# Dense projections on Trainium2: both parts of x as one operand of 512 columns, weights in 512 by 512 pieces

## The chip, the core and the metric

The kernel runs on one core of one Trainium2 chip. The time is the device time of one execution in microseconds (us); the median of several runs is compared. A core has a matrix engine (TensorE, PE in the profile, with its weight loads as PEld), a vector engine (VectorE, DVE), a scalar engine (ScalarE, ACT), GpSimd (POOL) and SyncE (SP), which issues nearly all DMAs here. Each engine works through a queue of its own in order and waits where another engine, or a DMA, has not yet delivered.

## What is computed

A trunk of two layers over x of 256 tokens by 1024 channels, float32 throughout. Each layer is a mixer and a feed-forward part, each followed by a residual and a layer norm:

```python
for l in range(DEPTH):                       # 2 layers
    h = x @ w_in[l]                          # 1024 -> 2304 columns
    q, k, v, u, xr, xg = jnp.split(h, IN_SPLITS, axis=-1)   # 512, 512, 512, 256, 256, 256
    y_attn = _diff_attention(q, k, v, lam, ...)             # 4 heads, softmax of two maps, p0 - lam * p1
    y_pool = _pool_mixer(u, pool_w[l], pool_scale[l])       # windows of 2, 4, 8 and 16
    y_lru = _rglru_mixer(xr, xg, ...)                       # convolution, gated scan, times gelu(xg)
    mix = jnp.concatenate([y_attn, y_pool, y_lru], axis=-1) @ w_out[l]
    x = _layer_norm(alpha * x + mix, ln1_g[l], ln1_b[l])
    if l % 2 == 0:
        f = _swiglu(x, ffn_w_gate, ffn_w_up, ffn_w_down)    # 1024 -> 2816 -> 1024
    else:
        f = _moe_swiglu(x, router_w, ...)                   # 8 experts of that size, 2 for each token
    x = _layer_norm(alpha * x + f, ln2_g[l], ln2_b[l])
```

## The kernel before

A float32 product is made of three products in a faster number type of the matrix engine (fp32r). Every operand is kept as two parts: `hi`, the value rounded to that type, and `lo`, what is left of it. A product is hi by hi, plus lo by hi, plus hi by lo; `mm3` issues these three matmuls. A weight tile comes by DMA as `raw`; `weight` makes `hi` with a ScalarE copy (L112) and `lo` with a VectorE subtraction (L114), for half a tile of 128x1024 at a time. x stands turned (channels on the partitions, 256 tokens along the row) in two tiles, `xh` and `xl`, made by `new_xT`.

A mixer goes in this order: values (`project_values`, which for layer 0 is `project_first_values`), then seven calls of `project` for 256 columns of `w_in` each: the recurrent channels xr, two for the queries (qT), two for the keys (kT), the gate branch xg and the pooling channels up. `project` takes two blocks c of 128 columns; for each block it goes over eight k (128 channels each) and issues `mm3` with the weights as the fixed operand and x as the moving one, 256 columns wide (L144, L145, L146). The two blocks share one PSUM bank, and one ScalarE copy of 128x512 brings the result to SBUF. Values and the first two chunks of the feed-forward part use `project_rows`: here x is the fixed operand, for 128 tokens t, and the weights move, 256 columns at a time.

Around the projections of the mixer stand the recurrent gates and the scan; the scores `sc` (L437; b is the block of 128 queries, and for b = 0 all four heads of one map fit in one bank of 128x512); the softmax (mask L451, row maximum L452, its scaling `nm` L453, exponentials on ScalarE L455, the ratio of the two maps L459 to L461, the difference `pr` L463); the turning of the probabilities (L504, copied by ScalarE as `pT`, L505) and their product with the values (L509); the gelu of xg on VectorE and ScalarE (L418 to L423); then the pooling sums and the output projection.

The feed-forward part of layer 0 (`dense_ffn`) has 11 chunks of 256 columns: two by `rows_part`, nine by `up_part`, where silu and the product of gate and up read PSUM. Layer 1 streams the weights of eight experts, 277 MB, through a ring of raw tiles, and a part of them is asked for while the mixer of layer 1 is still at work.

The order of the work is made by a scheduler when the program is built: it gives each engine its queue, from the order of the code, the data and the buffers. Pools of few buffers bound it: `mmp` has three PSUM banks for projections, `accp` four (scores and output projection), `tpp` one; the raw ring has five tiles at first, the split parts six or eight.

## Time and profile before

| | us |
|---|---|
| runs | 1109.02, 1110.88, 1113.15 |
| median | 1110.88 |
| the profiled execution, its own time | 1113.36 |
| its span, first to last instruction | 1111.6 |
| PE busy | 1067.3 (96%) |
| weight loads busy | 788.6 (71%) |
| DVE busy | 654.5 (59%) |
| ACT busy | 518.6 (47%) |
| mean granted TensorE clock | 0.977 of full |
| DMA | 346.9 MB, 312 GB/s |

The busy shares are means over stages that differ. In the order of time: from 0 to about 108 us the mixer of layer 0; to about 300 us the feed-forward part, in which PE has no gap; to about 400 us the mixer of layer 1; then the router, and from 420 us on the experts, in which the DMA engines are busy all the time. A row of a timeline is a start, a duration, the engine, the line of the program, the operation, what it writes and reads, and its form; in brackets stands the idle time ahead of it and what ended that. A matmul's duration holds its way through the array, and the next one starts earlier, so the pace of a stream of matmuls is read from starts.

### The profile page before, as it was taken

The numbers are of one execution on the slowest core, as the hardware profiler recorded it, in microseconds if no ns is written. First come the engines' busy times: TensorE is split into PE (matmuls) and PEld (weight loads), VectorE is DVE, ScalarE is ACT, GpSimd is POOL, SyncE is SP. The second block draws the span as 40 slices with busy tenths as digits, with TensorE's granted clock in tenths as the row PEclk, the third lists the DMA queues.
The fourth block names the chain that finished last, engine by engine and source line by source line (L and its number), as shares of the span: only waits on it lengthen the run. The fifth ranks groups of instructions, "written<-read, shape, count | busy, mean of one in ns | idle before, by whom it ended". The sixth has DMA issues, their size and how long they took to land. (4 is left out here: it accounts for less than half of the span.)

```text
span 1111.6 us, 15280 instructions
## 1 busy us (share of the span) xinstructions
PE 1067.3 (96%) x5866; PEld 788.6 (71%) x5867; DVE 654.5 (59%) x869; ACT 518.6 (47%) x722; POOL 24.8 (2%) x65
## 2 busy tenths in 40 slices
PE   8989999999998999999999999999999999999994
PEld 8977999999898883467873347884346884355883
DVE  6777744554777650169862049872138892137896
ACT  5865444444457330156651046761036772135773
POOL 1001000000100100000000000000000000000000
PEclk9989999999998969999999999999999999999998
DMA  9733755555473728999999999999999999999951
GB/s 311 291 112 113 265 168 181 190 184 189 127 263 141 261 117 350 414 413 413 409 419 419 414 414 412 406 419 398 386 414 411 409 420 371 374 412 412 411 208 41
DMA packets 152546, 346.91 MB, mean 312 GB/s; under 512 B 8196, under 2 KB 57488, under 8 KB 152464
## 3 DMA queue, kind: packets, MB, share of 16 engines
q1 hardware_dynamic: 152288, 345.56, 81.6%
q8 instruction: 48, 0.79, 0.3%
q14 instruction: 34, 0.28, 0.1%
q10 hardware_dynamic: 144, 0.26, 0.1%
q0 software_dynamic: 32, 0.02, 0.0%
HBM read 344.77 MB, written 1.05 MB: 311 GB/s over the span
## 5 line engine op out<-in xcount | busy, mean ns | idle before, releaser
L114 DVE TENSOR_TENSOR lo<-raw,hi 128x1024 fp32r<-128x1024 f32 x380 | 446.8, 1221 | 143.8 <-ACT hi L112 143.2
L112 ACT CAST hi<-raw 128x1024 fp32r<-128x1024 f32 x380 | 375.9, 1049 | 124.5 <-issue 54.3
L144 PE MATMUL mm<-xh,hi 128*128 128x256 f32 x512 | 147.1, 288 | 0.0
L145 PE MATMUL mm<-xh,lo 128*128 128x256 f32 x512 | 146.0, 285 | 0.0
L146 PE MATMUL mm<-xl,hi 128*128 128x256 f32 x512 | 146.0, 285 | 0.0
L1004 DVE TENSOR_TENSOR sg<-pu,sg 128x512 f32<-128x512 f32 (+2 forms) x36 | 23.3, 647 | 164.4 <-PE pu L976 137.8
L959 PE MATMUL pg<-hi,xg 128*128 128x512 f32 (+1 forms) x384 | 97.0, 378 | 4.7 <-ACT hi L112 4.7
L144 PEld LDWEIGHTS mm<-xh,hi 128*128 128x128 f32 x512 | 99.5, 195 | 0.9
L145 PEld LDWEIGHTS mm<-xh,lo 128*128 128x128 f32 x512 | 99.6, 194 | 0.4
L146 PEld LDWEIGHTS mm<-xl,hi 128*128 128x128 f32 x512 | 99.4, 194 | 0.0
L959 PE MATMUL pu<-hi,xg 128*128 128x512 f32 (+1 forms) x384 | 95.0, 373 | 0.0
L1028 PE MATMUL py<-hi,hT 128*128 128x512 f32 x344 | 92.9, 392 | 0.0
L976 PE MATMUL pg<-raw,xs 128*64 128x512 f32 (+1 forms) x384 | 86.2, 571 | 0.0
L976 PE MATMUL pu<-raw,xs 128*64 128x512 f32 (+1 forms) x384 | 84.3, 561 | 0.0
L959 PEld LDWEIGHTS pg<-hi,xg 128*128 128x128 f32 x384 | 68.4, 190 | 22.0 <-ACT hi L112 8.1
L998 PE MATMUL py<-raw,hs 128*64 128x512 f32 x352 | 79.9, 598 | 0.0
L959 PEld LDWEIGHTS pu<-hi,xg 128*128 128x128 f32 x384 | 68.3, 189 | 13.5 <-issue 0.7
L1003 ACT ACTIVATE sg<-pg 128x512 f32<-128x512 f32 (+2 forms) x36 | 20.3, 563 | 118.5 <-PE pg L976 69.6
L1028 PEld LDWEIGHTS py<-hi,hT 128*128 128x128 f32 x344 | 64.0, 188 | 13.6
L976 PEld LDWEIGHTS pg<-raw,xs 128*64 128x64 f32 x384 | 26.3, 139 | 44.8 <-issue 41.7
L976 PEld LDWEIGHTS pu<-raw,xs 128*64 128x64 f32 x384 | 26.2, 137 | 43.9 <-issue 41.6
L961 PE MATMUL pg<-lo,xg 128*128 128x512 f32 (+1 forms) x192 | 56.6, 383 | 0.6 <-DVE lo L114 0.4
(297 smaller groups left out, 1271.4 us busy)
## 6 DMA issues: line engine op xcount, KB each, us to landing
raw<-in_moe_w_down_dram SPq DMA_DIRECT2D x87, 1024.0 KB, 12.9
raw<-in_moe_w_gate_dram SPq DMA_DIRECT2D x76, 1024.0 KB, 14.2
raw<-in_moe_w_up_dram SPq DMA_DIRECT2D x76, 1024.0 KB, 13.6
raw<-in_w_in_dram SPq DMA_DIRECT2D x17, 1024.0 KB, 5.5
raw<-in_moe_w_gate_dram SPq DMA_DIRECT2D x16, 768.0 KB, 9.4
raw<-in_moe_w_up_dram SPq DMA_DIRECT2D x16, 768.0 KB, 8.3
raw<-in_ffn_w_gate_dram SPq DMA_DIRECT2D x11, 1024.0 KB, 5.1
raw<-in_ffn_w_up_dram SPq DMA_DIRECT2D x11, 1024.0 KB, 5.2
```

The lines of the kernel that those rows point to most:

```text
L112: act.copy(hi, raw[:, s, :])
L114: last_lo[:] = [vec.tensor_sub(lo, raw[:, s, :], hi.bitcast(F32))]
L144: pe.matmul(ps, lh, rh, start=first, stop=False)
L145: pe.matmul(ps, ll, rh, start=False, stop=False)
L146: return pe.matmul(ps, lh, rl, start=False, stop=last)
L959: pe.matmul(ps[:, :n], xg[i][:, k0 + k, :], w[k][0], start=(k0 + k + i == 0), stop=False)
L961: pe.matmul(ps[:, :n], xg[0][:, k0 + k, :], w[k][1], start=False, stop=(k0 + k == KD - 1))
L976: pe.matmul(ps[h * HALF:(h + 1) * HALF, :n], xs[:, k0 + k, :], raw[:, k, h * n:(h + 1) * n], start=(k0 + k == 0), stop=(k0 + k == KD - 1))
L998: pe.matmul(py[nn * HALF:(nn + 1) * HALF, :], hs[:, k % nk, k // nk, :], raw[:, k - k0, nn * 512:(nn + 1) * 512], start=(f + k == 0), stop ...
L1003: act.activation(sg[:, :n], pg[:, :n], AF.Silu)
L1004: vec.tensor_mul(sg[:, :n], pu[:, :n], sg[:, :n])
L1028: pe.matmul(ps, hT[i][:, k0 + k, :], w[k][0][:, s], start=(first and i == 0), stop=False)
```

## The change

`new_xT` makes one tile `x2`, with hi and lo of x beside each other for each k. `project` now issues two matmuls where it had three: the weight's hi part against the 512 columns [hi | lo] of x, and the weight's lo part against the 256 columns of x's hi. Both land in one bank of 128x512 for each block c: the left half takes hi by hi and lo by hi, the right half takes hi by lo. The two halves have to be added: a ScalarE copy of the right half (128x256) to the destination, then a VectorE addition of the left half to it. So a call of `project` takes two banks in turn instead of one, and ends with two copies and two additions instead of one copy. In `up_part` silu and the product with the up half now read SBUF, and a tile `su` is added.

`project_rows` takes weights 512 columns wide and half of the channels (`k0`) at a call. The weight pieces for values and for the first chunks are 512 rows by 512 columns instead of 1024 by 256, so a DMA row is 2 KB instead of 1 KB, at the same bytes for a piece. Counted over the program: 32 calls of `project` had 1536 matmuls of 256 columns, and have 512 of 512 columns and 512 of 256; `project_rows` had 384 of 256 columns and has 192 of 512. The 64 blocks have 64 copies and 64 additions. The layer norm's factors `g_b` of layer 1 take a tile of the raw ring where they had the place of `xl`.

```diff
     def new_xT():
-        return (const.tile([P, KD, T], F32R, tag="xh", name="xh"), const.tile([P, KD, T], F32R, tag="xl", name="xl"))
-
-    def project(src, c0, w=None):
+        x2 = const.tile([P, KD, 2, T], F32R, tag="x2", name="x2")
+        return x2[:, :, 0, :], x2[:, :, 1, :], x2
+
+    def project(src, c0, dst, w=None):
 
         w = w or weight(cols(src, c0, 256))
-        ps = mmp.tile([P, 2, T], F32, tag="mm", name="mm")
         for c in range(2):
             s = slice(c * P, (c + 1) * P)
+            ps = mmp.tile([P, 2, T], F32, tag="mm", name="mm")
             for k in range(KD):
-                mm3(ps[:, c, :], part(w[k], s), (xT[0][:, k, :], xT[1][:, k, :]), k == 0, k == KD - 1)
-        return ps
-
-    def project_rows(ps, w, t):
+                hi = lambda: pe.matmul(ps, w[k][0][:, s], xT[2][:, k, :, :], start=(k == 0), stop=(k == KD - 1))
+                lo = lambda: pe.matmul(ps[:, 0, :], w[k][1][:, s], xT[0][:, k, :], start=False, stop=False)
+                for product in (hi, lo) if k < KD - 1 else (lo, hi):
+                    product()
+            act.copy(dst[:, c, :], ps[:, 1, :])
+            last = vec.tensor_add(dst[:, c, :], ps[:, 0, :], dst[:, c, :])
+        return last
+
+    def project_rows(ps, w, t, k0):
 
         tok = slice(t * P, (t + 1) * P)
-        for h in range(0, KD, KD // 2):
-            ks = range(h, h + KD // 2)
-            for k in ks:
-                for i in range(2):
-                    pe.matmul(ps, xT[i][:, k, tok], w[k][0], start=(k + i == 0), stop=False)
-            for k in ks:
-                mm = pe.matmul(ps, xT[0][:, k, tok], w[k][1], start=False, stop=(k == KD - 1))
+        ks = range(KD // 2)
+        for k in ks:
+            for i in range(2):
+                pe.matmul(ps, xT[i][:, k0 + k, tok], w[k][0], start=(k0 + k + i == 0), stop=False)
+        for k in ks:
+            mm = pe.matmul(ps, xT[0][:, k0 + k, tok], w[k][1], start=False, stop=(k0 + k == KD - 1))
         return mm
 ...
             for t in range(NT):
-                ps = mmp.tile([P, 2, 256], F32, tag="mm", name="mm")
-                for c in range(2):
-                    mm = project_rows(ps[:, c, :], w[c], t)
+                ps = mmp.tile([P, ATT], F32, tag="mm", name="mm")
+                for i in range(2):
+                    mm = project_rows(ps, w[i], t, 4 * i)
                 if t == 0:
                     hold[:] = [turn_last(mm)]
-                act.copy(v[:, t, :], ps.rearrange("p a b -> p (a b)"))
+                act.copy(v[:, t, :], ps)
 ...
+                w = weight(cols(w_in[l][0:4 * P, :], 2 * ATT, ATT), True)
...
+            project_rows(ps[0], w, 0, 0)
...
         def qk(dst, c0, c):
-            act.copy(dst[:, 2 * c:2 * c + 2, :], project(w_in[l], c0 + 256 * c, S.pop(("w", c0 + 256 * c), None)))
+            project(w_in[l], c0 + 256 * c, dst[:, 2 * c:2 * c + 2, :], S.pop(("w", c0 + 256 * c), None))
...
-            act.copy(xg, ps)
+            project(w_in[l], 2048, xg, S.pop(("w", 2048), None))
...
-            return act.copy(up[:, :, PAD:], ps)
+            return project(w_in[l], 1536, up[:, :, PAD:], S.pop(("w", 1536), None))
...
-        g_t, b_t = gb(ln1_g, ln1_b, l, const.tile([P, 2, D], F32, tag="xl", name="g_b") if l == DEPTH - 1 else None)
+        g_t, b_t = gb(ln1_g, ln1_b, l)
...
     def ffn_piece(i):
-        return weight(cols((ffn_w_gate, ffn_w_up)[i % 2][0], 256 * (i // 2), 256))
+
+        return weight(cols((ffn_w_gate, ffn_w_up)[i // 2][0][4 * P * (i % 2):4 * P * (i % 2 + 1), :], 0, 512))
 
...
         def up_part(j):
-            pg = project(ffn_w_gate[0], 256 * j)
             sg = tmp(j % 2, [P, 2, T], "sg")
-            act.activation(sg, pg, AF.Silu)
-            pu = project(ffn_w_up[0], 256 * j)
-            vec.tensor_mul(sg, pu, sg)
+            project(ffn_w_gate[0], 256 * j, sg)
+            act.activation(sg, sg, AF.Silu)
+            su = tmp(4 + j % 2, [P, 2, T], "su")
+            project(ffn_w_up[0], 256 * j, su)
+            vec.tensor_mul(sg, su, sg)
...
             ws = list(begun)
             for t in range(NT):
+                ps = [mmp.tile([P, 512], F32, tag="mm", name="mm") for _ in range(2)]
+                for i in range(4):
+                    if len(ws) == i:
+                        ws.append(ffn_piece(i))
+                    mm = project_rows(ps[i // 2], ws[i], t, 4 * (i % 2))
+                    if t == 0 and i == 2:
+                        turn_last(mm)
                 for j in range(2):
-                    ps = mmp.tile([P, 2, 256], F32, tag="mm", name="mm")
-                    for i in (2 * j, 2 * j + 1):
-                        if len(ws) == i:
-                            ws.append(ffn_piece(i))
-                        mm = project_rows(ps[:, i % 2, :], ws[i], t)
-                        if t == 0 and i == 2:
-                            turn_last(mm)
-                    rows_h(t, j, ps)
+                    rows_h(t, j, [p_[:, 256 * j:256 * (j + 1)] for p_ in ps])
 
...
```

The queues change with it. First ScalarE's queue, in the mixer of layer 0, from the first block or call of the second keys (kT) to the exponentials of b = 0 (L455; names and numbers after an underscore are tiles). Before:

```order
L365 COPY kT<-mm 128x512 [waits PE_49]
L112 CAST hi<-raw 128x1024
L455 ACT_TABLE_LOAD [waits DVE_49]
L455 ACTIVATE pr,rs__746<-sc,nm 128x128 [waits PE_49]
L455 ACTIVATE pr,rs__746<-sc,nm 128x128 x3
L112 CAST hi<-raw 128x1024 [waits DMAHW2_49,PE_49]
L455 ACTIVATE pr,rs__746<-sc,nm 128x128 [waits DVE_49]
L455 ACTIVATE pr,rs__746<-sc,nm 128x128 x3
L413 COPY xg<-mm 128x512 [waits PE_49,Activation_49]
L112 CAST hi<-raw 128x1024
L455 ACTIVATE pr,rs__794<-sc,nm 128x256 [waits DVE_49,PE_49]
```

After, the same stretch:

```order
L228 COPY kT<-mm 128x256 [waits PE_49]
L112 CAST hi<-raw 128x1024
L228 COPY xg<-mm 128x256 [waits PE_49,Activation_49]
L112 CAST hi<-raw 128x1024 [waits DMAHW2_49,PE_49]
L228 COPY xg<-mm 128x256 [waits PE_49]
L112 CAST hi<-raw 128x1024
L458 ACT_TABLE_LOAD
L458 ACTIVATE pr,rs__625<-sc,nm 128x128 [waits DVE_49]
L458 ACTIVATE pr,rs__625<-sc,nm 128x128 x3
L458 ACTIVATE pr,rs__625<-sc,nm 128x128 [waits DVE_49]
L458 ACTIVATE pr,rs__625<-sc,nm 128x128 x3
```

The copies of xg stood behind the exponentials of b = 0 and now stand ahead of them, each followed by a cast of a weight's hi part; the load of the exponential's table stands behind all of these.

VectorE's queue at the same place, from the mask of the scores of b = 0 (`MEMSET sc`). Before:

```order
L451 MEMSET sc 64x4x64 [waits PE_49]
L452 TENSOR_REDUCE nm<-sc 128x4 [waits DVE_49]
L451 MEMSET sc 64x4x64 [waits PE_49]
L453 TENSOR_SCALAR nm<-nm 128x4 [waits DVE_49]
L452 TENSOR_REDUCE nm<-sc 128x4 [waits DVE_49]
L453 TENSOR_SCALAR nm<-nm 128x4 [waits DVE_49]
L114 TENSOR_TENSOR lo<-raw,hi 128x1024 [waits DMAHW2_49,Activation_49]
L451 MEMSET sc 64x2x64 [waits PE_49]
L459 RECIPROCAL ratio<-rs__746 128x4 [waits Activation_49]
```

After:

```order
L454 MEMSET sc 64x4x64 [waits PE_49] x2
L455 TENSOR_REDUCE nm<-sc 128x4 [waits DVE_49]
L114 TENSOR_TENSOR lo<-raw,hi 128x1024 [waits DMAHW2_49,Activation_49]
L455 TENSOR_REDUCE nm<-sc 128x4 [waits DVE_49]
L456 TENSOR_SCALAR nm<-nm 128x4 [waits DVE_49]
L229 TENSOR_TENSOR xg<-mm,xg 128x256 [waits Activation_49]
L114 TENSOR_TENSOR lo<-raw,hi 128x1024 [waits Activation_49]
L456 TENSOR_SCALAR nm<-nm 128x4 [waits DVE_49]
L421 TENSOR_TENSOR gl<-xg 128x512 [waits DVE_49]
L422 TENSOR_SCALAR gl<-gl 128x512 [waits DVE_49]
L423 TENSOR_TENSOR gl<-gl,xg 128x512 [waits DVE_49]
L462 RECIPROCAL ratio<-rs__625 128x4 [waits Activation_49]
```

Between the first maximum (`TENSOR_REDUCE`) and the second scaling `nm` there now stand two subtractions `lo` and the addition of xg's second block, and three steps of the gelu stand ahead of the ratio, where they were spread behind it.

Third, ScalarE's queue in the mixer of layer 1, from the end of the first map's exponentials of b = 0 to the copy of pT. Before:

```order
L112 CAST hi<-raw 128x1024 [waits DMAHW6_49,PE_49]
L455 ACTIVATE pr,rs__3568<-sc,nm 128x128 [waits DVE_49]
L455 ACTIVATE pr,rs__3568<-sc,nm 128x128 x3
L413 COPY xg<-mm 128x512 [waits PE_49,Activation_49]
L112 CAST hi<-raw 128x1024
L455 ACTIVATE pr,rs__3616<-sc,nm 128x256 [waits DVE_49,PE_49]
L455 ACTIVATE pr,rs__3616<-sc,nm 128x256
L505 COPY pT<-tp 128x512 [waits PE_49]
```

After:

```order
L112 CAST hi<-raw 128x1024
L458 ACTIVATE pr,rs__3028<-sc,nm 128x128 [waits DVE_49]
L458 ACTIVATE pr,rs__3028<-sc,nm 128x128 x3
L424 ACTIVATE gl<-gl 128x512 [waits DVE_49]
L458 ACTIVATE pr,rs__3076<-sc,nm 128x256 [waits DVE_49,PE_49]
L458 ACTIVATE pr,rs__3076<-sc,nm 128x256
L458 ACTIVATE pr,rs__3076<-sc,nm 128x256 [waits DVE_49,PE_49]
L458 ACTIVATE pr,rs__3076<-sc,nm 128x256
L458 ACTIVATE pr,rs__3076<-sc,nm 128x256 [waits DVE_49,PE_49]
L458 ACTIVATE pr,rs__3076<-sc,nm 128x256
L507 COPY pT<-tp 128x512 [waits PE_49]
```

The copy of xg has left this stretch (both of its blocks stand ahead of the table load, as in layer 0), and of the first exponentials of b = 1 (128x256) three groups of two stand ahead of the copy of pT where one stood.

## Rows read from the trace of the kernel before

**Rows 1.** Busy us by stretch: PE, PEld, DVE, ACT, POOL; granted clock, DMA share, GB/s

```profile
150.00:300.00 150.00, 149.94 (x1036) 140.08 (x1035) 79.30 (x83) 64.28 (x71) 2.13 (x4) 1.00 0.55 179
400.00:420.00 20.00, 18.99 (x76) 15.15 (x78) 8.33 (x46) 4.83 (x10) 1.02 (x12) 0.53 0.00 0
420.00:1071.00 651.00, 635.58 (x2993) 394.49 (x2990) 360.68 (x386) 291.84 (x361) 0.00 (x0) 1.00 1.03 405
```

**Rows 2.** TensorE timeline: start, duration, engine, line, operation; feed-forward projection in layer 0

```profile
200.47 0.28 PE L144 MATMUL mm<-xh,hi 128*128 128x256 f32 x1
...
204.43 0.28 PE L144 MATMUL mm<-xh,hi 128*128 128x256 f32 x1
```

**Rows 3.** TensorE timeline, output projection of layer 1

```profile
379.07 0.39 PE L145 MATMUL acc<-hi,mixl 128*128 128x512 f32 x1
...
381.56 0.39 PE L144 MATMUL acc<-hi,mixh 128*128 128x512 f32 x1
```

**Rows 4.** TensorE timeline, start of layer 0's pooling projection, and that stretch as in 1

```profile
70.87 0.41 PE L145 MATMUL mm<-xh,lo 128*128 128x256 f32 x1
...
71.08 0.41 PE L146 MATMUL mm<-xl,hi 128*128 128x256 f32 x1
...
70.87:73.64 2.77, 2.77 (x15) 2.77 (x14) 1.79 (x6) 2.51 (x10) 0.00 (x0) 0.50 0.94 329
```

**Rows 5.** Operations by line, by form: 128x256 reads of PSUM (count | busy, mean ns | idle)

```profile
L130 ACT CAST hT<-tp 128x256 fp32r<-128x256 f32 x4 | 1.5, 369 | 0.7 <-PE tp L658 0.7
...
L655 DVE TENSOR_TENSOR sg<-mm,sg 128x256 f32<-128x256 f32 x4 | 1.7, 421 | 1.9 <-ACT sg L654 1.9
```

**Rows 6.** ScalarE timeline, layer 0's softmax

```profile
58.87 1.28 ACT L455 ACT_TABLE_LOAD   x1 [3.65 <-DVE nm L453]
...
60.17 0.37 ACT L455 ACTIVATE pr<-sc,nm 128x128 f32<-128x128 f32 x1
...
61.56 1.05 ACT L112 CAST hi<-raw 128x1024 fp32r<-128x1024 f32 x1
...
63.87 0.62 ACT L413 COPY xg<-mm 128x512 f32<-128x512 f32 x1
...
68.14 0.59 ACT L505 COPY pT<-tp 128x512 f32<-128x512 f32 x1 [0.50 <-PE tp L504]
...
71.66 0.46 ACT L455 ACTIVATE pr<-sc,nm 128x256 f32<-128x256 f32 x1
```

**Rows 7.** VectorE timeline, the same place

```profile
57.72 0.69 DVE L452 TENSOR_REDUCE nm<-sc 128x4 f32<-128x512 f32 x1
...
59.49 0.17 DVE L453 TENSOR_SCALAR nm<-nm 128x4 f32<-128x4 f32 x1
...
62.64 1.22 DVE L114 TENSOR_TENSOR lo<-raw,hi 128x1024 fp32r<-128x1024 f32 x1 [2.98 <-ACT hi L112]
...
65.60 0.67 DVE L418 TENSOR_TENSOR gl<-xg 128x512 f32<-128x512 f32 x1
...
66.48 1.10 DVE L463 SCALAR_TENSOR_TENSOR pr<-pr,ratio 128x128 f32<-128x128 f32 x4
```

**Rows 8.** TensorE timeline, the same place

```profile
61.02 1.99 PE L437 MATMUL sc<-kT,qT 64*128 64x256 f32 x12
...
66.84 1.26 PE L504 MATMUL tp<-ident,pr 128*128 128x128 f32 x4 [1.64 <-DVE pr L463]
...
68.78 2.07 PE L509 MATMUL mm<-v,pT 128*128 128x128 f32 x8 [0.68 <-ACT pT L505]
```

**Rows 9.** ScalarE and TensorE timelines, layer 1's softmax

```profile
346.61 1.28 ACT L455 ACT_TABLE_LOAD   x1 [3.65 <-DVE nm L453]
...
351.61 0.62 ACT L413 COPY xg<-mm 128x512 f32<-128x512 f32 x1
...
348.76 1.99 PE L437 MATMUL sc<-kT,qT 64*128 64x256 f32 x12
...
356.51 2.07 PE L509 MATMUL mm<-v,pT 128*128 128x128 f32 x8 [0.68 <-ACT pT L505]
```

More of the change, by code (lines that the diff above doesn't have):

```diff
@@ L347, in project_first_values @@
                 pe.transpose(warm[:, 0, :], ident, ident)
-            ps = [mmp.tile([P, 2, 256], F32, tag="mm", name="mm") for t in range(NT)]
-            _, split = transposed_split(x_nat[:, 0, :], *xT, 0, True)
+            ps = [mmp.tile([P, ATT], F32, tag="mm", name="mm") for t in range(NT)]
+            _, split = transposed_split(x_nat[:, 0, :], *xT[:2], 0, True)
             with after(*split):
-                w = weight(cols(w_in[l], 2 * ATT, 256), True)
+                w = weight(cols(w_in[l][0:4 * P, :], 2 * ATT, ATT), True)
             nc.sync.dma_start(x_nat[:, 1, :], x[P:2 * P, :])
-            project_rows(ps[0][:, 0, :], w, 0)
-            _, split = transposed_split(x_nat[:, 1, :], *xT, 1, True)
+            project_rows(ps[0], w, 0, 0)
+            _, split = transposed_split(x_nat[:, 1, :], *xT[:2], 1, True)
             with after(*split):
-                w1 = weight(cols(w_in[l], 2 * ATT + 256, 256))
-            project_rows(ps[1][:, 0, :], w, 1)
+                w1 = weight(cols(w_in[l][4 * P:8 * P, :], 2 * ATT, ATT))
+            project_rows(ps[1], w, 1, 0)
             for t in range(NT):
-                project_rows(ps[t][:, 1, :], w1, t)
+                project_rows(ps[t], w1, t, 4)
                 if t == 1:
                     params()
-                act.copy(v[:, t, :], ps[t].rearrange("p a b -> p (a b)"))
+                act.copy(v[:, t, :], ps[t])
         def qk(dst, c0, c):
-            act.copy(dst[:, 2 * c:2 * c + 2, :], project(w_in[l], c0 + 256 * c, S.pop(("w", c0 + 256 * c), None)))
+            project(w_in[l], c0 + 256 * c, dst[:, 2 * c:2 * c + 2, :], S.pop(("w", c0 + 256 * c), None))
         def recurrent_in():
-            ps = project(w_in[l], 1792, S.pop(("w", 1792), None))
             S["xr"] = xr = tmp(0, [P, 2, 3 + T], "xr")
             gp.memset(xr[:, :, 0:3], 0.0)
-            act.copy(xr[:, :, 3:], ps)
+            project(w_in[l], 1792, xr[:, :, 3:], S.pop(("w", 1792), None))
         def convolution():
@@ L410, in recurrent_out @@
         def recurrent_out():
-            ps = project(w_in[l], 2048, S.pop(("w", 2048), None))
             S["xg"] = xg = tmp(0, [P, 2, T], "xg")
-            act.copy(xg, ps)
+            project(w_in[l], 2048, xg, S.pop(("w", 2048), None))
         def recurrent_gelu():
@@ L467, in pooling @@
         def pooling():
-            ps = project(w_in[l], 1536, S.pop(("w", 1536), None))
             PAD = 16
@@ L672, in dense_ffn @@
         ws = [weight(rows(ffn_w_down[0], 2 * j, 2)) for j in js]
-        begun[:] = [weight(cols(w_in[1], 2 * ATT + 256 * i, 256)) for i in range(2)]
+        begun[:] = [weight(cols(w_in[1][4 * P * i:4 * P * (i + 1), :], 2 * ATT, ATT)) for i in range(2)]
         begun_lo = last_lo[0]
@@ L777, in route @@
         if t == 0:
-            xn.extend(const.tile([P, NT, D], F32R, tag=nm, name="xn") for nm in ("xh", "xl"))
+            parts = const.tile([P, 2, NT, D], F32R, tag="x2", name="xn")
+            xn.extend(parts[:, i, :, :] for i in range(2))
             marks[:] = [normed]
@@ L1183, in trunk @@
     overflow()
-    normed = const.tile([P, NT, D], F32, tag="xh", name="normed")
+    normed = const.tile([P, 2, NT, D], F32, tag="x2", name="normed")[:, 0, :, :]
     rs = mot.tile([P, NT], F32, tag="rs", name="rs")
```

8 lines of the change are left out of this document (4 added, 4 removed).

## The prediction

> **What bounds the kernel now.** I read the busy time by stretch first [rows 1]. In the feed-forward part of layer 0 PE is busy for 149.94 of 150 us, with DVE at 79.30, ACT at 64.28 and the DMA engines at a share of 0.55: there PE alone sets the pace. From 420 us on the DMA engines stand at a share of 1.03 and move 405 GB/s: the experts are bound by their weights. Between them, from 400 to 420 us, the share is 0.00: what was asked for ahead has landed, and the stream goes on only when PE frees its first tile. So the experts' part keeps its length, and a microsecond gained or lost before it moves the end by a microsecond. The order of SP's queue supports that: 13 tiles of expert weights are issued ahead of the load that waits for the chosen experts, before and after.
>
> In the mixers PE waits, and the timelines of the two softmaxes show for whom [rows 6 to 9]. PE's scores of b = 1 start at 61.02, right behind xg's projection; its transpose starts at 66.84, after 1.64 us of idling for DVE's `pr`, and the product with the values at 68.78, after 0.68 for ACT's copy [rows 8]. Layer 1 repeats this, with 348.76 and 356.51 for the first and last of these starts [rows 9].
>
> **Fewer matmuls.** The pace is read from starts. 256 columns: 33 steps from 200.47 to 204.43, 0.120 us each [rows 2]. 512 columns: 11 steps from 379.07 to 381.56, 0.2264 us [rows 3]. The difference, 0.1064 us, is what 256 columns more take, so a matmul has 0.0136 us that do not depend on its width. Three of 256 take 0.360 us, one of each kind takes 0.3464: 0.0136 us less for each block and k, 16 times that, 0.218 us, for a call of `project`. Right after PE has idled in the softmax its granted clock is 0.50, the lower of its two levels (1.2 GHz), and two starts lie 0.21 us apart [rows 4]: the columns alone, twice 0.1064. There I count no gain; those stretches are short.
>
> The Trainium skill speaks against this sum: "TensorE: Matmul & The Clock Gate", section "Back-to-back issue gap", gives the gap of a warm matmul as its columns over 2.4 plus about 2.5 ns. An estimate by that page for the 704 matmuls that go (512 in `project`, 192 in rows) is 1.8 us, where the trace's 0.0136 gives 9.6. The trace's two paces disagree with the page on the constant, and I go by the trace.
>
> What lies on the path: 18 calls in `up_part`, 18 x 0.218 = 3.9 us. The first chunks' rows, 192 matmuls to 96: 96 x 0.0136 = 1.3. Values, 96 to 48 in each layer: 0.65 each, 1.3. In each mixer three calls ahead of the gates, 0.65 each, 1.3, and the pooling call, 0.2 each, 0.4. Together 8.2 us. (The three calls between gates and softmax are in the walk below.) Wider DMA rows may help the start of layer 0 a little; as nothing here prices it, it goes into the range, from 0 to 0.5.
>
> **New evictions where PE is the bound.** A block ends with a ScalarE copy of 128x256, about 0.37 us, and an addition of 128x256, about 0.42 [rows 5]. A chunk of `up_part` gets four of each, 1.7 us of DVE and 1.5 of ACT, less the work that no longer reads PSUM. A chunk is 96 matmuls of 0.120 and 24 of 0.2264 of its down product, 17 us; DVE and ACT are about half free there [rows 1]. A block's bank is wanted again after two more blocks, 2 x 8 x 0.346 = 5.5 us; copy, addition and one hi cast and one lo ahead of them are 0.37 + 0.42 + 1.05 + 1.22 = 3.1 us [rows 5 to 7]. So nothing is charged. If that cover were gone, each block would cost what it exceeds 5.5 us.
>
> **The softmax of layer 0.** Here the queues are the matter, as the order rows of the change show: both copies of xg and the casts behind them now stand ahead of the exponentials of b = 0 on ACT, and two lo splits, xg's addition and three gelu steps ahead of the ratio on DVE. I walk it with the durations of the rows, on the clock of the trace before. xg's projection ended at 61.02. Eight of the 256-wide score matmuls now stand ahead of that point: 1.99/12 x 8 = 1.33 us more; three calls give back 0.65: 61.7. Then ACT: copy 0.37, cast 1.05, table load 1.28, so the exponentials begin at 64.4 instead of 60.17. Two groups of four of 1.39 us (60.17 to 61.56): 67.2 instead of 63.87, 3.3 late [rows 6]. The gelu steps on DVE are done by then. From there DVE: three reciprocals and a ratio, three scalings and a mask at about 0.17, three maxima at 0.69, one gelu step at 0.67 [rows 7], nearly 4 us by durations and about 3.2 by starts, as DVE's operations overlap somewhat: `pr` begins at 70.4 to 71.1. Before it began at 66.48, and the product with the values 2.30 us later (68.78). So that product begins at 72.7 to 73.4: 3.9 to 4.6 late. The order may resolve somewhat better than a walk by single steps, so I take **3.8 us**, with 1.5 and 5.5 as ends.
>
> **The softmax of layer 1.** The same, with a cast between the groups of exponentials. xg's end 348.76 + 1.33 - 0.65 = 349.44; copy 0.37 and table load 1.28: 351.1, against 346.61 + 1.28 before. Exponentials, cast, exponentials: 1.39 + 1.05 + 1.39, end at 354.9, where it was 351.61 [rows 9]. Then three maxima, a gelu step and the small steps, 3.2 to 4.0 us, until `pr` at 358.4 (lo's in between are hidden by the exponentials). On ACT six of the 256-wide exponentials, 0.46 each [rows 6], stand ahead of the copy of pT and start with their `nm`, just before `pr`: 358.3 + 2.8 = 361.1, then the copy, and the product 0.64 later (68.14 to 68.78 in layer 0): 361.7. Before: 356.51, so 5.2 late. Taken with the same reserve: **5.0 us**, ends 2.5 and 7.
>
> After that product the pooling call follows at once in both orders, and pr of b = 1 comes while it runs. Its own eviction is copy plus addition (0.79) where one copy of 0.6 was [rows 6]: 0.1 us for each layer, 0.2 together.
>
> **The sum.** -8.2 + 3.8 + 5.0 + 0.2 = +0.8 us. The profiled execution took 1113.36 us (span 1111.6), 2.5 above the median; the terms do not depend on that, so 1114.2 for such an execution and **1111.7** against the median of 1110.88.
>
> **The rivals.** A change of 0.5%, 5.6 us, is about the least that a measurement of this kernel can tell from none.
>
> *The waits do not grow.* In both softmaxes PE idles already, and the additions may slip into gaps that DVE has (2.98 us before the lo of 62.64) [rows 7]. Against it: the exponentials stand behind xg's copy in the queue, whatever DVE does. With the low ends, 1.5 + 2.5, the sum is -4.0; with no growth at all -8: 1103 to 1107. The faster half of this is over the bound. Together with a start that gains from wider rows, 27 in 100 for over 5.6 us faster.
>
> *Softmax costs more.* One mechanism: each mixer's PE stands idle so long that its clock falls for longer. It is granted 1.2 GHz at the start of the pooling call now [rows 4], after idling of 1.64 and 0.68 [rows 8]; a whole call at that level takes 48 x 0.213 = 10.2 us where it takes 48 x 0.120 = 5.8 at full clock; about 15 of the 48 are slow already, so up to 3 us more. With the walk's high ends, 5.5 and 7, and 2 us of clock for each layer: -8.2 + 12.5 + 4 = +8.3, 1119. It decides from 5.6 us, or 14 us lost in the mixers together. 18 in 100.
>
> *The pair costs as much as the three.* Weight loads are busy for 140.08 of the 150 us [rows 1]; if what a matmul has beside its columns comes from its weight load, and a load beside a 256-column matmul cannot hide behind it, the constant may not go away with the third matmul. The gain is then between none and a fifth, 0 to 1.8 us, and the sum +7 to +9: 1118 to 1120. It decides when a pair takes over 0.355 us. For it: the loads are that dense. Against it: one load goes away with each matmul. By the skill's page named above, the gain would be the 1.8 us of its constant. 10 in 100.
>
> *It does not do what it says.* The order shows a 512-wide and a 256-wide matmul in turn in every call, so this has no weight.
>
> **How the numbers follow.** Same 45 in 100, from the sum and its ends around it (1106 to 1116); faster 27, slower 28. The range leaves out the far part of both sides: 1103, where the waits do not grow, to 1119, the colder softmax.
>
> **What would show it.** Starts in `up_part` going 0.226 and 0.120 apart, and the nine chunks 3.9 us shorter with no PE idling; the exponentials of b = 0 behind xg's copies, some 3 us late; the product with the values 3.8 and 5.0 us later after xg's scores than before; the first expert tile's release shifted by the sum of both, and the end by the same. It would be wrong if the pair's pace is not the sum of the two, if PE waits for a bank in `up_part`, or if the experts' part changes its length.

## The result and the profile after

The changed kernel takes **1122.59 us** (median of four runs, 1122.19 to 1125.01) where the kernel before took 1110.97 beside it: ratio 1.0116, 95% interval 1.0098 to 1.0134. It is slower, by 11.6 us, and outside the range. Its profiled execution took 1122.50 us (span 1120.8, mean granted clock 0.973), so the two traces differ by 9.2 us in their spans. The other 2.4 us are in the profiled execution of before, which was that much above its median.

Busy time by stretch, columns as in [rows 1]:

```profile
150.00:300.00 150.00, 149.94 (x781) 127.87 (x780) 93.25 (x116) 75.90 (x104) 3.14 (x5) 1.00 0.55 182
400.00:420.00 20.00, 17.84 (x79) 16.48 (x80) 11.15 (x54) 6.55 (x14) 1.02 (x12) 0.56 0.19 63
420.00:1071.00 651.00, 634.43 (x2974) 390.38 (x2975) 354.48 (x381) 286.46 (x357) 0.00 (x0) 1.00 1.02 403
```

In the feed-forward part PE has no gap, as before, with 781 matmuls where 1036 were, and DVE rose from 79.30 to 93.25: the new evictions are covered. The totals hide the loss; it shows when the trace is cut at events that both kernels have. Each part below runs from the start of one instruction to that of the next; `product` is the first product with the values, `LN1` and `LN2` the first transposes of a normed x, `down` the first down product, `sg2` and `sg5` the third and the sixth `sg` product of the experts, `mean` and `normed` the last `nmean` and the first last-norm step on DVE. The predicted column is the prediction's terms put into these parts; every other column is a difference from before (e1 to e12 are the runs of the next section), each kernel in its own profiled execution. So a column's sum need not be the difference of the medians: the execution of e11 was 1.8 us below the median of e11, that of before 2.4 above its own.

| part | before, us | predicted | after | e1 | e2 | e3 | e5 | e9 | e11 | e12 |
|---|---|---|---|---|---|---|---|---|---|---|
| start to product, layer 0 | 68.78 | +2.5 | +2.15 | -2.55 | +2.87 | -1.40 | +0.84 | +1.94 | -2.43 | -0.81 |
| to LN1 | 34.89 | -0.1 | -0.53 | +0.03 | -0.57 | +0.03 | -1.00 | +0.03 | +3.53 | -0.16 |
| to down (first chunks) | 40.40 | -1.3 | -0.88 | -1.69 | -0.35 | -1.18 | -1.70 | -0.88 | -1.60 | -0.01 |
| to LN2 (nine chunks) | 149.47 | -3.9 | -1.83 | -1.84 | 0.00 | 0.00 | -1.83 | -1.83 | -1.84 | 0.00 |
| to product, layer 1 | 62.98 | +3.7 | +4.80 | -0.69 | +4.79 | -0.84 | +2.84 | +1.76 | -1.00 | +0.01 |
| to LN1 | 35.88 | -0.1 | -0.06 | +0.37 | +0.36 | -0.58 | -0.24 | +1.27 | +2.86 | -0.10 |
| to sg2 (router) | 71.68 | 0 | +0.58 | +0.60 | +0.62 | -1.51 | +0.57 | +0.58 | -1.95 | 0.00 |
| to sg5 (first experts) | 61.22 | 0 | **+2.75** | -0.01 | -0.22 | +2.75 | -0.26 | -0.26 | 0.00 | +0.03 |
| to mean | 573.05 | 0 | +0.07 | -0.18 | +0.04 | -1.65 | +0.04 | -1.52 | -0.06 | -0.06 |
| to normed (tail) | 3.88 | 0 | **+2.10** | +0.38 | +0.16 | +0.27 | +0.35 | +0.33 | +0.19 | -0.02 |
| to the end | 9.38 | 0 | +0.05 | -0.02 | 0.00 | +0.01 | -0.01 | -0.02 | 0.00 | +0.02 |
| sum | 1111.6 | +0.8 | +9.2 | -5.6 | +7.7 | -4.1 | -0.4 | +1.4 | -2.3 | -1.1 |

The mixers lost in sum about what was forecast: their four parts sum to 6.36, forecast 6.0 (how much of that is luck is said below). The feed-forward part gave 2.71 of a forecast 5.2. And 5.55 us were lost behind LN1 of layer 1, where the forecast had nothing.

The softmax of layer 0 after, on ScalarE, VectorE and TensorE (timelines, columns as in [rows 6 to 8]):

```profile
60.18 0.37 ACT L228 COPY xg<-mm 128x256 f32<-128x256 f32 x1 [1.11 <-PE mm L224]
60.45 1.05 ACT L112 CAST hi<-raw 128x1024 fp32r<-128x1024 f32 x1
61.51 1.28 ACT L458 ACT_TABLE_LOAD   x1
62.81 0.37 ACT L458 ACTIVATE pr<-sc,nm 128x128 f32<-128x128 f32 x1
```

```profile
63.34 0.68 DVE L421 TENSOR_TENSOR gl<-xg 128x512 f32<-128x512 f32 x1
...
65.83 1.26 DVE L455 TENSOR_REDUCE nm<-sc 128x2 f32<-128x512 f32 x2
...
67.20 0.67 DVE L425 SCALAR_TENSOR_TENSOR gl<-gl,xg 128x512 f32<-128x512 f32 x1
...
68.62 1.10 DVE L466 SCALAR_TENSOR_TENSOR pr<-pr,ratio 128x128 f32<-128x128 f32 x4
```

```profile
64.36 3.46 PE L440 MATMUL sc<-kT,qT 64*128 64x256 f32 x8 [4.22 <-ACT pr L458]
68.99 1.26 PE L506 MATMUL tp<-ident,pr 128*128 128x128 f32 x4 [1.16 <-DVE pr L466]
70.93 2.08 PE L511 MATMUL mm<-v,pT 128*128 128x128 f32 x8 [0.67 <-ACT pT L507]
```

The exponentials stand behind xg's second copy, its cast and the table load, as forecast, and start at 62.81 where they started at 60.17 [rows 6]; then maxima and gelu steps stand ahead of `pr`, but they cost nothing on top: from the first exponential to `pr` it is 5.81 us, where it was 6.31 (60.17 to 66.48). In layer 0 the delay is the late start of the exponentials. PE, which had idled 1.06 ahead of the last scores (the row of before that follows) and then 1.64 and 0.68 [rows 8], now idles 4.22, 1.16 and 0.67.

```profile
64.07 1.13 PE L437 MATMUL sc<-kT,qT 64*128 64x256 f32 x4 [1.06 <-ACT pr L455]
```

Layer 1, ScalarE, VectorE and TensorE in the same way:

```profile
347.79 0.37 ACT L228 COPY xg<-mm 128x256 f32<-128x256 f32 x1 [0.48 <-PE mm L224]
348.18 1.28 ACT L458 ACT_TABLE_LOAD   x1
349.48 0.37 ACT L458 ACTIVATE pr<-sc,nm 128x128 f32<-128x128 f32 x1
...
359.56 0.61 ACT L507 COPY pT<-tp 128x512 f32<-128x512 f32 x1
```

```profile
356.90 1.10 DVE L466 SCALAR_TENSOR_TENSOR pr<-pr,ratio 128x128 f32<-128x128 f32 x4
```

```profile
357.27 1.26 PE L506 MATMUL tp<-ident,pr 128*128 128x128 f32 x4 [1.82 <-DVE pr L466]
360.22 2.08 PE L511 MATMUL mm<-v,pT 128*128 128x128 f32 x8 [1.69 <-ACT pT L507]
```

The copy of pT waits behind six 128x256 exponentials that start at 356.85, and PE waits 1.69 for it where it waited 0.68 [rows 9]. Counted from LN2, the 4.80 us of layer 1 are 2.67 of a later first exponential, 1.12 between it and `pr`, and 1.01 between `pr` and the product.

The waits of PE up to 455 us sum this up, after and then before (what waits, for what: us in total, times, longest):

```profile
PE sc L440 <- ACT pr L458: 7.2, 3, 4.2
PE mm L511 <- ACT pT L507: 3.4, 3, 1.7
PE tp L506 <- DVE pr L466: 3.0, 2, 1.8
```

```profile
PE tp L504 <- DVE pr L463: 3.3, 2, 1.6
PE mm L509 <- ACT pT L505: 2.3, 3, 1.0
PE sc L437 <- ACT pr L455: 2.1, 2, 1.1
```

13.6 us against 7.7, and nearly all of the growth is scores that wait for exponentials.

### The profile page after: what moved, and what is told of

Same layout as the page of the kernel before. It is cut to its first block, busy times and chain, and to the rows that moved or that the text cites. A ratio compares the mean times of both kernels' runs of the same rounds, so it can differ in the third digit from the quotient of the medians.

```text
span 1120.8 us, 13955 instructions
## 1 busy us (share of the span) xinstructions
PE 1066.2 (95%) x5162; PEld 750.5 (67%) x5163; DVE 677.0 (60%) x933; ACT 531.7 (47%) x772; POOL 23.3 (2%) x65
## 5 line engine op out<-in xcount | busy, mean ns | idle before, releaser
L114 DVE TENSOR_TENSOR lo<-raw,hi 128x1024 fp32r<-128x1024 f32 x380 | 446.4, 1220 | 108.7 <-ACT hi L112 107.8
L224 PE MATMUL mm<-x,hi 128*128 128x512 f32 x512 | 181.7, 402 | 0.3 <-DVE qT L229 0.3
L225 PE MATMUL mm<-x,lo 128*128 128x256 f32 x512 | 134.5, 283 | 0.0
L224 PEld LDWEIGHTS mm<-x,hi 128*128 128x128 f32 x512 | 94.4, 191 | 19.3 <-DVE qT L229 0.7
L225 PEld LDWEIGHTS mm<-x,lo 128*128 128x128 f32 x512 | 97.7, 191 | 5.7
L1033 PEld LDWEIGHTS py<-hi,hT 128*128 128x128 f32 x344 | 64.1, 188 | 13.6
L1035 PE MATMUL py<-lo,hT 128*128 128x512 f32 x172 | 55.6, 405 | 0.0
L966 PE MATMUL pu<-lo,xg 128*128 128x512 f32 (+1 forms) x192 | 55.4, 377 | 0.0
```

The costliest lines, as they stand in the source:

```text
L114: last_lo[:] = [vec.tensor_sub(lo, raw[:, s, :], hi.bitcast(F32))]
L224: hi = lambda: pe.matmul(ps, w[k][0][:, s], xT[2][:, k, :, :], start=(k == 0), stop=(k == KD - 1))
L225: lo = lambda: pe.matmul(ps[:, 0, :], w[k][1][:, s], xT[0][:, k, :], start=False, stop=False)
L966: pe.matmul(ps[:, :n], xg[0][:, k0 + k, :], w[k][1], start=False, stop=(k0 + k == KD - 1))
L1033: pe.matmul(ps, hT[i][:, k0 + k, :], w[k][0][:, s], start=(first and i == 0), stop=False)
L1035: pe.matmul(ps, hT[0][:, k0 + k, :], w[k][1][:, s], start=False, stop=last)
```

## The experiments

**Which part costs (e1 to e4).** e1 keeps the old `project` in the mixers and changes all else, e2 keeps it in `up_part`, e3 makes only the 512 by 512 pieces and rows in the kernel before, e4 moves only `g_b`, in the kernel before too. `project3` is the old `project`; e1's edit for xg stands for those of all the mixers' calls, e2's is like it in `up_part`.

```diff
-            project(w_in[l], 2048, xg, S.pop(("w", 2048), None))
+            ps = project3(w_in[l], 2048, S.pop(("w", 2048), None))
+            act.copy(xg, ps)
```

```diff
-        g_t, b_t = gb(ln1_g, ln1_b, l, const.tile([P, 2, D], F32, tag="xl", name="g_b") if l == DEPTH - 1 else None)
+        g_t, b_t = gb(ln1_g, ln1_b, l)
```

> The changed kernel, but the mixers' calls of project keep three matmuls of 256 columns (on the two halves of x2) and one copy of 128x512; the feed-forward part and the rows stay as changed. Theory 1 (the mixers lose in the softmax queues, the feed-forward part gains): the product with the values no longer late, 68.8 less about 1 us in layer 0 and 356.5 less about 4 in layer 1 (first rows of layer 1 at 294 to 296, then 59 us as before), so 6 to 8 us less than the changed kernel at the first expert tile. Rival (the loss is not in the mixers' evictions but in g_b's place or the rows): softmax times as in the changed kernel, within 1.5 us of it.

> The changed kernel, but up_part keeps three matmuls of 256 columns and reads PSUM; mixers and rows as changed. Theory 1: softmax as late as in the changed kernel (some 3 us in layer 0, near 5 in layer 1, counted from xg's projection), nine chunks at 16.98 us each instead of 16.72, so 2 to 3 us later than the changed kernel at the first expert tile. Rival (pace of a pair no better than the three, the gain of the chunks comes from elsewhere): chunks at 16.7 us still.

> The kernel before with the 512 by 512 pieces and 512-column rows alone; xh, xl, project and g_b as before. Theory 1: 96, 48 and 48 matmuls fewer, 1 to 3 us less ahead of the experts, softmax as before. The order of casts and subtractions among the first experts moves here too, although nothing there was edited; if that is what costs 2.8 us between 465 and 525 us in the changed kernel, it shows here; if the ring slot of g_b costs it, it does not show here.

> The kernel before with one edit: the layer norm's factors of layer 1 take a tile of the raw ring. If the ring slot costs the 2.8 us among the first experts (a weight tile asked for later): shift of 2.8 us between the first expert and the second, total 1113 to 1115. If it is the order of casts there, which moves here as in the changed kernel: the same shift, and also in the kernel with the rows alone. If neither: within 1 us of before. The dense part as before in all cases.

Measured: e1 1105.33 us, ratio 0.9947 (0.9930 to 0.9964); e2 1120.08, 1.0083 (1.0066 to 1.0100); e3 1107.75, 0.9977 (0.9965 to 0.9988); e4 1111.70, 1.0015 (1.0003 to 1.0027). So the pairs help in the feed-forward part and hurt in the mixers: the nine chunks are 1.84 shorter in e1 and unchanged in e2, the way to the product of layer 1 is 4.79 longer in e2 and shorter in e1. The first experts tell against `g_b`'s place: e1 and e2 have it in the ring and lose nothing there, e3 has it not and loses 2.75 between sg2 and sg5.

**The pair's pace (e7).** e1 with the eight narrow matmuls of a block behind each other instead of one after each wide one.

```diff
+            hi = lambda k: pe.matmul(ps, w[k][0][:, s], xT[2][:, k, :, :], start=(k == 0), stop=(k == KD - 1))
+            hi(0)
             for k in range(KD):
-                hi = lambda: pe.matmul(ps, w[k][0][:, s], xT[2][:, k, :, :], start=(k == 0), stop=(k == KD - 1))
-                lo = lambda: pe.matmul(ps[:, 0, :], w[k][1][:, s], xT[0][:, k, :], start=False, stop=False)
-                for product in (hi, lo) if k < KD - 1 else (lo, hi):
-                    product()
+                pe.matmul(ps[:, 0, :], w[k][1][:, s], xT[0][:, k, :], start=False, stop=False)
+            for k in range(1, KD):
+                hi(k)
```

> The kernel with the change in the feed-forward part alone, with the eight 256-column matmuls of a block in a row, between the first and the second of 512 columns. If turning from one width to the other is what costs 6 ns in each pair (0.3525 us instead of 0.3464 from the two paces), nine chunks of 16.72 us become 16.55 (16 x 2 x 6 ns less), 1.7 us in all. If a 512-column matmul takes the longer step whatever stands before it, the chunks stay at 16.72.

The changed kernel's call in `up_part`, first and last wide starts and what follows, from TensorE's timeline, and then e7's:

```profile
200.68 0.39 PE L224 MATMUL mm<-x,hi 128*128 128x512 f32 x1
200.91 0.28 PE L225 MATMUL mm<-x,lo 128*128 128x256 f32 x1
201.02 0.40 PE L224 MATMUL mm<-x,hi 128*128 128x512 f32 x1
...
211.96 0.40 PE L144 MATMUL acc<-hi,hT 128*128 128x512 f32 x1
```

```profile
195.53 2.00 PE L223 MATMUL mm<-x,hi 128*128 128x512 f32 x8
197.37 1.12 PE L226 MATMUL mm<-x,lo 128*128 128x256 f32 x8
198.33 0.63 PE L223 MATMUL mm<-x,hi 128*128 128x512 f32 x2
```

Between 200.68 and 211.96 lie two calls, 32 pairs: 0.3525 us for a pair, where the sum of the two paces is 0.3464 and three narrow ones take 0.360. In e7 a wide one takes 1.84/8 = 0.230 and a narrow one 0.96/8 = 0.120, and the nine chunks are 2.69 shorter than before instead of 1.83. A chunk takes 16.61, between the two forecasts. So some of the missing gain goes with the alternation; the rest (3.9 less 2.69, 1.2) stays, and most of it is the wide matmul itself, at 0.230 here instead of the 0.2264 of the output projection [rows 3]: 288 x 0.0036 = 1.0. e7 takes 1105.18 us, ratio 0.9944 (0.9919 to 0.9969): with e1 the fastest of the study, and faster than both kernels.

**What delays the softmax (e5, e6, e9, e11).** e6 evicts xg alone in the old way. e5 leaves the additions of the mixers' calls out, and with them the part hi by lo of these projections. e9 keeps them and holds the softmax of b = 1 and the gelu of xg behind `pr` of b = 0. e11 does what e5 and e9 do. First e5's edit (the mixers' calls pass `add=False`), then e9's.

```diff
-            act.copy(dst[:, c, :], ps[:, 1, :])
-            last = vec.tensor_add(dst[:, c, :], ps[:, 0, :], dst[:, c, :])
+            last = act.copy(dst[:, c, :], ps[:, 1 if add else 0, :])
+            if add:
+                last = vec.tensor_add(dst[:, c, :], ps[:, 0, :], dst[:, c, :])
```

```diff
-        softmax(0)
+        mixed = softmax(0)
...
-        softmax(1)
-        recurrent_gelu()
+        with after(mixed):
+            softmax(1)
+            recurrent_gelu()
```

> The changed kernel with xg alone projected as before (three matmuls of 256, one copy of 128x512). In layer 0 that copy still stands ahead of the exponentials, in layer 1 it stands among them, behind seven of eight. If xg's eviction ahead of the exponentials is what costs, layer 1's product gains 3 us or more on the changed kernel and layer 0's at most 1. If the additions to qT and kT (scores wait for them) are what costs, both stay within 1.5 us of the changed kernel.

> The changed kernel without VectorE's additions in the two mixers: a block's copy takes the left half of the bank, and the right half (hi of the weight by lo of x) is left out of the result; matmuls, banks and copies stay. If the additions on VectorE, and what waits for them, make the softmax late: the products with the values come as in the kernel with the old mixers (66.2, and 62.3 us after layer 1's first rows), some 8 us less than the changed kernel at the first expert tile. If the split copies and the order in ScalarE's queue do it (xg's first copy and the table load still stand ahead of the exponentials): less than 4 of the 10 us come back.

> The changed kernel with one rule of order more: the softmax of b = 1 and the gelu steps come behind pr of b = 0. Theory: of the 4.7 and 5.4 us that the mixers lose, the part behind the exponentials is VectorE's maxima and gelu steps ahead of pr, and in layer 1 six exponentials ahead of the copy of pT; pr should follow the end of the exponentials by some 1 us instead of 3.1 and 3.8, and the product come 2 to 3 us earlier in layer 0 and 3 to 4 in layer 1. If the later part (b = 1) then comes late, that is given back before the output projection ends. Rival (PE is bound by something else there): product within 1 us of the changed kernel. Among the first experts ScalarE's casts stand here in the order of before, so the 2.8 us between 465 and 525 us should be gone, whatever g_b's place (it is in the ring).

> The changed kernel with both edits that gave a part of the mixers' loss back: the additions in the mixers' seven calls of project are left out with hi by lo (the destination takes the left half alone, so the part hi by lo of these projections is left out of what is computed), and the softmax of b = 1 and the gelu of xg stand behind pr of b = 0. The pooling call keeps its shape, also without the addition. Theory: the loss of the mixers is made of two things that add up, DVE's and ACT's order around pr of b = 0, and the evictions with their additions. Then the product with the values starts where it did with the mixer of before (run e1_ffn_only: 66.23 in layer 0, and 62.28 after LN2's first transpose in layer 1): 66 to 67.5 and 62 to 63.5. Rival: each edit takes the same wait away, so that together they give no more than the better one (69.6 or 70.7 in layer 0, 64.7 in layer 1): 69 or more, 64 or more. In the order the casts of the second gathered tile do not stand ahead of the first expert's weights, so from sg2 to sg5 (before: 61.22) within 0.4 us of before. Time: theory 1106 to 1110, rival 1110 to 1114.

e6: 1124.73 us, 1.0121 (1.0090 to 1.0153); its way to the product of layer 1 is 4.95 longer than before, after's 4.80. The form of xg's eviction is not the cause. Nor is its place in layer 1: in e6 xg's copy stands there behind seven of the eight exponentials, and they still start 56.35 after LN2 (57.03 in the changed kernel, 54.36 before). e5: 1113.81, 1.0032 (1.0013 to 1.0051), +2.84 there. e9: 1113.02, 1.0016 (0.9995 to 1.0036), +1.76. So each gives back a part in layer 1. In layer 0, counted from the first call of `project`, where the changed kernel is 4.71 us longer than before, e5 gives back 0.81 and e9 nothing (0.33 longer), while e8, of the same order there, differs by 1.04. The times of e5 and e9 can't be put down to the mixers alone: behind LN1 of layer 1, where they edit nothing, their traces are 4.9 and 6.4 us shorter than that of the changed kernel.

e11: 1112.81, 1.0026 (1.0014 to 1.0037), and there the product starts at 66.35 and 61.97 after LN2, where e1, with the old calls, has 66.23 and 62.28. From e11's timelines of ScalarE, VectorE and TensorE, and then e1's of the first two:

```profile
60.27 0.37 ACT L459 ACTIVATE pr<-sc,nm 128x128 f32<-128x128 f32 x1
```

```profile
64.03 1.11 DVE L467 SCALAR_TENSOR_TENSOR pr<-pr,ratio 128x128 f32<-128x128 f32 x4
```

```profile
66.35 2.07 PE L513 MATMUL mm<-v,pT 128*128 128x128 f32 x8 [0.68 <-ACT pT L509]
```

```profile
57.63 0.37 ACT L470 ACTIVATE pr<-sc,nm 128x128 f32<-128x128 f32 x1
```

```profile
63.93 1.10 DVE L478 SCALAR_TENSOR_TENSOR pr<-pr,ratio 128x128 f32<-128x128 f32 x4
```

`pr` begins 3.76 after the first exponential, in the changed kernel 5.81 (62.81 to 68.62), in e1 6.30. So e11 does not take the delay away. Its exponentials still start 2.64 later than e1's, without the additions (2.50 in layer 1, from LN2), and the order around `pr` makes that up with a stretch shorter than the mixers of before had. Nor do the two edits simply add up: in layer 0 they give the product 1.31 and 0.21 alone and 4.58 together, in layer 1 1.96, 3.04 and 5.80. What the rest of the late exponentials comes from (the split copies, or the order that came with them) no run separates. And the held work has to be done: product to LN1 is 3.53 and 2.86 longer in e11, little of the gain arrives, and its time lies in the range of its rival. A cure by order alone was not found.

**Both, in one kernel (e10).** e7 with e9's order.

> The feed-forward change with the eight narrow matmuls in a row, old mixers, and the same rule of order. If the rule helps old mixers too: products 1 to 2 us earlier than in the kernel without it. Here the casts among the first experts stand in the other order (a second cast of xg ahead of the first weight's cast), so 2 to 2.8 us should be lost between 465 and 525 us; together about the same as without the rule, 1104 to 1107.

1116.05 us, 1.0047 (1.0025 to 1.0068), where 1104 to 1107 was expected. The product of layer 0 comes at 64.00, the earliest of all, and LN1 at 103.62, 3.4 later than in e7. In a mixer whose softmax is not late, holding work behind it costs more behind the product than it gives ahead of it; the first experts cost 2.83 and the tail 2.31 on top. (The profiled execution, 1112.75, was the fastest of the six.)

**The tail, and how much is scatter (e8, e12).** e8 puts 16 tiny memsets at the start of DVE's program; e12 is the kernel before once more.

```diff
-    vec.reciprocal(few, few)
+    vec.reciprocal(few, few); pad = midt.tile([P, 1], F32, tag="pad", name="pad"); _ = [vec.memset(pad, 0.0) for _ in range(16)]
```

> The changed kernel with 16 tiny memsets more at the start of VectorE's queue, where it is idle; the order of everything else is the same. If the 2.1 us that the changed kernel loses between the last mean and the last normalisation is where VectorE's code lies when it jumps over the overflow part, that gap (5.98 us; 3.88 before) goes back toward 4 us and the total falls by about 2. If it belongs to the work there, the gap stays.

> The kernel of before, unchanged, profiled a second time: what does the same program do from one execution to the next? Theory: the steps that the study rests on are set by the queues, so the two transposes of pr and the two products with the values (68.78, 356.51), the pace of the first experts (sg2 to sg5 61.22) and the 3.88 from the last mean to normed come again within 0.3 us, and the span moves by up to 2 us through the start of layer 0 and the clock. Rival: any of them moves by a microsecond or more from execution to execution; then what was read from single profiles (the 2.1 us of the tail, the 2.8 of the first experts) has to be taken as scatter.

DVE's timeline at the end: after, e8, e12.

```profile
1105.39 0.21 DVE L1090 TENSOR_SCALAR nmean<-sums 128x1 f32<-128x1 f32 x1
1111.37 2.74 DVE L1195 SCALAR_TENSOR_TENSOR normed<-x_nat,nmean,raw 128x512 f32<-128x512 f32 x4 [5.77 <-issue]
```

```profile
1107.14 0.21 DVE L1090 TENSOR_SCALAR nmean<-sums 128x1 f32<-128x1 f32 x1
...
1111.28 1.41 DVE L1195 SCALAR_TENSOR_TENSOR normed<-x_nat,nmean,raw 128x512 f32<-128x512 f32 x2 [3.93 <-DVEq L1174]
```

```profile
1097.24 0.21 DVE L1085 TENSOR_SCALAR nmean<-sums 128x1 f32<-128x1 f32 x1
1101.10 2.74 DVE L1190 SCALAR_TENSOR_TENSOR normed<-x_nat,nmean,raw 128x512 f32<-128x512 f32 x4 [3.65 <-DVEq L1169]
```

With the same work, e8's tail is 4.14 instead of 5.98. Between the two instructions DVE goes past the overflow part, which is in the program but not run (line 1169 or 1174 is its branch). So in this one trace most of the 2.1 us went with where DVE's program stands, not with what it does. That it is the fetch of the code behind the branch fits, but no wait shows it. The profile's DMA rows bear on it. Packets of a queue of kind `instruction` (q14) come in this gap, after and then in e8:

```profile
q14 instruction: 4, 0.03, 2.0%
```

```profile
q14 instruction: 2, 0.02, 1.0%
```

In the three kernels with a gap of about 6 us (the changed one, e6 and e10) such a packet starts 1.7 to 1.9 us ahead of `normed`, as if DVE waited for it; in the other eleven it starts 0.26 to 0.29 behind. The rows do not say for which engine it comes, so this is not shown. e8's total, 1122.04 us (ratio 1.0093, 1.0057 to 1.0129), is not the 2 us better that were expected: to LN1 of layer 0 its trace lost 1.2 against the changed kernel, 0.5 of it ahead of the product; the clock from 72 to 80 us was 0.71 of full where that had 0.84.

e12: 1111.25 us, ratio 1.0003 (0.9988 to 1.0018). Ten of its parts come again within 0.16 us, those of the first experts and the tail within 0.03; the start moves by 0.81, with one wait of PE for a tile of x in either, 0.25 us for the first in e12 and 0.85 for the second in before. So, by this one repeat, what was read from single profiles stands, except for about a microsecond in layer 0.

**The first experts.** No run was made for these alone, but the kernels sort themselves by one place in the order. ScalarE's timeline there, after and before:

```profile
468.81 0.37 ACT L871 CAST xg<-ps_g 128x256 fp32r<-128x256 f32 x1 [1.38 <-PE ps_g L868]
473.43 0.37 ACT L871 CAST xg<-ps_g 128x256 fp32r<-128x256 f32 x1 [4.25 <-PE ps_g L868]
473.70 1.99 ACT L112 CAST hi<-raw 128x1024 fp32r<-128x1024 f32 x2
```

```profile
464.58 0.37 ACT L866 CAST xg<-ps_g 128x256 fp32r<-128x256 f32 x1 [1.38 <-PE ps_g L863]
468.18 1.99 ACT L112 CAST hi<-raw 128x1024 fp32r<-128x1024 f32 x2 [3.23 <-DMA raw<-in_moe_w_gate_dram]
470.92 0.37 ACT L866 CAST xg<-ps_g 128x256 fp32r<-128x256 f32 x1 [0.75 <-PE ps_g L863]
```

After, the second cast of the gathered `xg` stands ahead of the first weights' `hi`, and waits 4.25 us for a gather that PE has behind 16 down products. Kernels with that order (after, e3, e4, e6, e8, e10) lose 2.13 to 2.83 between sg2 and sg5, the others (e1, e2, e5, e7, e9, e11, e12) between -0.26 and +0.03. For e9, e10 and e11 the side was named before they ran. The stream of weights goes on, after its pause, with the fourteenth tile that SP asks for, before and after:

```profile
419.07 0.37 SPq L973 DMA_DIRECT2D raw<-in_moe_w_up_dram  x1
```

```profile
423.29 0.38 SPq L978 DMA_DIRECT2D raw<-in_moe_w_up_dram  x1
```

From its request to sg5 the kernels with that order take 108.7 to 109.8 us, the others 106.0 to 106.3. But this is not yet the length of the experts' part. In e3, e4, e9 and e10 some 1.6 us come back in one step, at the 22nd `sg` product, for a reason that no run shows. So from LN1 of layer 1 to the mean the changed kernel, e6 and e8 are 3.3 to 3.5 longer than before, while e3, e4 and e10, with the same order of casts, are 0.4, 0.4 and 1.3 shorter, and e9, without it, 1.2.

The stream itself is not what is late there. Windows of before and after, shifted by the 4.23 that sg2 is later:

```profile
610.00:630.00 20.00, 19.14 (x98) 7.01 (x96) 1.44 (x2) 1.77 (x3) 0.00 (x0) 1.00 1.03 417
464.07:494.07 30.00, 30.00 (x150) 18.00 (x150) 15.48 (x18) 14.05 (x19) 0.00 (x0) 1.00 1.04 412
```

```profile
614.23:634.23 20.00, 19.14 (x92) 6.60 (x90) 2.69 (x4) 1.77 (x3) 0.00 (x0) 1.00 0.99 376
468.30:498.30 30.00, 30.00 (x144) 17.02 (x144) 12.90 (x15) 11.91 (x17) 0.00 (x0) 1.00 1.04 412
```

In the first 30 us both move 412 GB/s, but PE does 6 matmuls less. The stream pays only at 614 us, with 376 GB/s instead of 417, or (417 - 376) x 20 / 412 = 2.0 us of transfer. PE's idling that the trace shows there is 1.17 us, for a `lo`; how the rest of the 2.75 comes about inside PE's queue is open. So is the router's +0.58 (-1.03 to -2.51 in e3, e4, e10, e11); it lies ahead of the request at 423.29.

## Why the prediction was wrong

- **"So the experts' part keeps its length"** is the step that failed: 5.55 of the 8.4 us by which the sum of terms and the traces differ lie behind LN1 of layer 1. The row that it rested on has PE busy for 635.58 of 651 us [rows 1], 98%: PE was as near its bound as the DMA engines, so a worse order of PE's and ScalarE's queues can cost time though the stream is full. From the request with which the stream goes on (423.29 and 419.07) to the last mean it is 682.10 us after and 679.27 before: 2.8 longer, where the step has 0. Of the order there only SP's queue was compared; the scheduler moved ScalarE's casts and PE's gathers as well, though the diff touches nothing of the experts, and it does so for an edit as small as e4's. That this order is the cause rests on how the kernels sort, since no run moved it alone; the 2.10 of the tail, part of the 5.55, does not come from it (e8 has the same order and a tail of 4.14).
- **The pair's pace**, -3.9, was mis-sized: the nine chunks gave 1.83. The paces of two unmixed streams were added [rows 2, 3]; mixed, a pair takes 0.3525, nearly in the middle between 0.3464 and 0.360. With the 0.3525 the term is 18 x 16 x 0.0075 = 2.2; the nine chunks show 2.1 of it, as two transposes of the first chunks (0.25 us) moved into this part. The Trainium skill, "TensorE: Matmul & The Clock Gate", section "Back-to-back issue gap", has 2.5 ns beside a matmul's columns; estimated from it, 288 matmuls less would give 0.7 us. The trace's 1.83 lies between that and the forecast.
- **The rows**, -1.3, gave 0.88, 0.25 of it those transposes (1.18 in e3, where they did not move).
- **The softmaxes** were right in kind and too small in size. Against e1, which has the old calls there, the product is 4.70 and 5.49 us late. The forecast for that is 3.15 and 4.35 (3.8 and 5.0, less 0.65 for the three calls ahead of the gates), with upper ends of 4.85 and 6.35. That layer 0 comes out at +2.15 for a forecast of +2.5 is luck: the first call of `project` starts 2.57 earlier than before (20.32 against 22.88), where 0.65 and up to 0.5 were forecast and e12 shows a scatter of 0.82, and from there the product is 4.71 later. In layer 0 the eight scores were forecast ahead of xg's end; they came behind it, at 64.36, which shortened the way to the exponentials and lengthened the idling after them. In layer 1 the step to the copy of pT behind six exponentials came as walked.
- **New evictions at nothing** was right: no wait of PE in `up_part`.
- **The rivals.** "Waits do not grow" fell. "Pair costs as much" named the right term and half its size. "Softmax costs more", by the clock, has its time, 1119, near the result for another reason: from the product to LN1 the changed kernel is 0.53 and 0.06 shorter than before, so no net cost of a colder clock shows there.
- **The tail**, 2.10, was in no term. The trace of before has 3.88 there and nothing that tells that it can grow.

## What to carry over

A kernel whose order a scheduler makes changes in places that the diff doesn't touch: compare the order of every engine to the end, above all where two engines are both near their bound, before a part is said to keep its length; and compare parts, not only times, since here several microseconds came and went where no edit was. A pace is taken from the mix that will run, not from the sum of two pure streams. Fewer matmuls that need one more eviction pay where PE alone is the bound (e1 0.9947 and e7 0.9944, of which the rows alone give 0.9977 in e3) and cost where PE already waits for ScalarE and VectorE, so in this kernel they belong in the feed-forward part alone.

## What the runs showed of the hardware

A 512-column matmul in turn with a 256-column one takes 0.3525 us a pair, 0.0061 more than the two in streams of their own (0.2264 and 0.120); eight of each in a row take 0.230 and 0.120 (e7). And DVE's way past a part that isn't run took 3.88 us before and 5.98 after, with the same work; 16 tiny instructions at the start of its program brought the 5.98 to 4.14.
